# A 3x3 convolution in Winograd form: the first pair's store issued three PSUM copies later, and seven rows stored apart in another pair

## The chip, the cores and the metric

The kernel runs on one core of one Trainium2 chip. The time is the device time of one launch in microseconds (us), the median of several runs. A profile is one more execution, taken by the hardware profiler; its span runs from the core's first instruction to its last.

The names of the engines are those of the profile: PE (TensorE, matmuls), PEld (its weight loads), DVE (VectorE), ACT (ScalarE), POOL (GpSimd) and SP (SyncE). A "q" behind a name (SPq, ACTq) stands for that engine's sequencer, which waits and issues DMAs.

## What is computed

A convolution of 16 images with 64 input channels of 64 x 64 pixels, with a 3 x 3 kernel, a border of one zero pixel and 128 output channels, all in float32 in DRAM:

```python
batch, c_in, h, w, c_out = 16, 64, 64, 64, 128
x_pad = np.pad(x, ((0, 0), (0, 0), (1, 1), (1, 1)), mode='constant')
...
output[b, co] += weight[co, ci, kh, kw] * x_pad[b, ci, kh:kh+h, kw:kw+w]
```

The input is 16.8 MB, the output 33.6 MB, the weights 0.3 MB.

## The kernel before, in words

**Work and tiles.** Two images make a pair: 2 x 64 input channels fill the 128 partitions, and there are eight pairs. Each pair is computed in two halves (h = 0 and 1) of 32 output rows, so the main loop (L206) has 16 passes, n = 0 to 15. A half uses four PSUM tiles (pf1, pg1, pf2, pg2), which hold the vertical Winograd sums for 16 row pairs, in two blocks of eight. Three of them are copied to SBUF by ScalarE (`copied`, L180, recorded at L182: ux, ug, uy), ScalarE then casts the next half's rows to 16 bits (`cast`, L122, recorded at L124), VectorE makes three of the four output parts (L231 to L233), and ScalarE copies the fourth (L234). GpSimd makes the input sums and differences of the half after the next (`transforms`, L208; recorded at L106, L113 and L119).

**Homes.** One SBUF tile, `homes`, has nine slots of 16 KB per partition. An input pair takes one (X_HOME, L49), an output pair takes two that lie side by side, one for each of its images (O_HOME, L50). Pair 0's output lies in slots 5 and 6, which pair 3's output takes again, and later pair 6's. Pair 1's output lies in slots 3 and 4, which pair 4's takes again.

**DMAs.** SP issues the weights (L58), then the loads of pair 0 in two cuts, of pairs 1 and 2, and of pairs 3 and 4 in one DMA of 4096 KB (L68 to L72). The loads of pairs 5, 6 and 7 come later, behind the first halves of pairs 2, 3 and 4 (NEXT_LOADS, L53 and L237), because they need slots whose earlier inputs have been read. The output of a pair is stored by `store` (L187) once its second half is done. Pairs 0, 3 and 6 (BOTH, L51) are stored by one DMA of 4096 KB; the others by one DMA of 2048 KB for each image. ScalarE issues the store of pair 0 and SP all others. For one image, named by FEW (L52), the last seven rows are stored apart: one DMA for the first 57 rows of all 128 channels (1824 KB), one for the last seven rows of 124 channels (217 KB) and one for those of the last four channels (7 KB). In the kernel before this is pair 5, image 1 of the pair.

**What sets the order.** Every instruction is wrapped in `keep`, so each engine runs its instructions in the order of the program. An issue of a DMA stands in its engine's queue like any other instruction: it first waits for its data (for a store, the last of L231 to L234), and what stands behind it on that engine waits as well. In the kernel before ScalarE's queue reads, around the store of pair 0: the copy of L234 for n = 1, the issue at L192, then the three copies of L182 and the cast for n = 2. Within SP's queue the DMAs stand in this order: weights, five loads, the stores of pair 1, load 5, the stores of pair 2, load 6, the store of pair 3, load 7, the stores of pairs 4, 5, 6 and 7. The completion semaphores of all DMAs, ScalarE's among them, are eight, used in turn in program order: a DMA also waits until the one eight places before it has landed.

Of the kernel before, what the change touches and what calls it, by code (L numbers as in the profile page):

```python
# [15 lines left out]
def kernel(  # L16
# [32 lines left out]
    X_HOME = [0, 1, 2, 7, 8, 2, 7, 8]  # L49
    O_HOME = [5, 3, 0, 5, 3, 0, 5, 2]  # L50
    BOTH = (0, 3, 6)  # L51
    FEW = 5, 1, 7  # L52
    NEXT_LOADS = {(2, 0): 5, (3, 0): 6, (4, 0): 7}  # L53
    homes = slots.tile([128, 9, H, W], F32)
    xs = [homes[:, k, :, :] for k in X_HOME]
# [4 lines left out]
    def load(p, cuts=((0, H),)):  # L60
        for lo, hi in cuts:
            keep(
                nc.sync.dma_start(
                    xs[p][:, lo:hi, :], x_rows[128 * p : 128 * p + 128, lo:hi, :]
                )
            )
# [55 lines left out]
    def cast(p, h):  # L122
        t = cpool.tile([128, 17, W], F16, tag="xh", name="xh")
        keep(nc.scalar.copy(t, xs[p][:, C_ROW[h] : C_ROW[h] + 17, :]))  # L124
        return t

    def transforms(eng, p, h):
        return sums(eng, p, h), diffs(eng, p, h), outers(eng, p, h)
# [17 lines left out]
    def mms(tiles, terms, start, stop):  # L146
        n = 3 * len(terms)
        i = 0
        for wi, src, row in terms:
            for kw in (1, 0, 2):  # L150
                c_lo, c_hi = max(0, 1 - kw), min(W, W + 1 - kw)
                lo, hi = 0, RB
                at, step, rows = row
                while at + step * lo < 0:
                    lo += 1
                while at + step * (hi - 1) > rows - 1:
                    hi -= 1
                first, last = at + step * lo, at + step * (hi - 1)
                for b2 in range(2):
                    p0 = 64 * b2  # L160
                    keep(
                        nc.tensor.matmul(  # L162
                            tiles[:, b2, lo:hi, c_lo:c_hi],
                            Wt[p0 : p0 + 64, wi, kw, :],
                            src[
                                p0 : p0 + 64,
                                first : last + 1 : step,
                                c_lo + kw - 1 : c_hi + kw - 1,
                            ],
                            start=start and i == 0,  # L170
                            stop=stop and i == n - 1,
                            skip_group_check=not start,
                        )
                    )
                i += 1

    def acc():
        return psum.tile([128, 2, RB, W], F32, tag="acc", name="acc")

    def copied(tiles):  # L180
        ut = upool.tile([128, 2, RB, W], F32, tag="ut", name="ut")
        keep(nc.scalar.copy(ut, tiles))  # L182
        return ut
# [3 lines left out]
    def store(p, both):  # L187
        if p in BOTH:
            pair = out[2 * p : 2 * p + 2, :, :, :].rearrange("b c h w -> c b h w")

            eng = nc.scalar if p == 0 else nc.sync
            keep(eng.dma_start(pair, both))  # L192
            return
        for b2 in range(2):
            parts = [(0, CO, 0, H)]
            if (p, b2) == FEW[:2]:
                at = H - FEW[2]
                parts = [(0, CO, 0, at), (0, 124, at, H), (124, 4, at, H)]
            for c, n, lo, hi in parts:
                keep(  # L200
                    nc.sync.dma_start(
                        out[2 * p + b2, c : c + n, lo:hi, :], both[c : c + n, b2, lo:hi, :]
                    )
                )

    for n, (p, h) in enumerate(halves):  # L206
        if n + 2 < len(halves):
            tr[halves[n + 2]] = transforms(nc.gpsimd, *halves[n + 2])  # L208
        if h == 0:
            both = homes[:, O_HOME[p] : O_HOME[p] + 2, :, :]  # L210
            ov = both.rearrange("p b (j i) c -> p b j i c", i=2)
        ss, dd, ee = tr.pop((p, h))
        xc = xh.pop((p, h))
        jf, jg = RB * F_BLK[h], RB * G_BLK[h]
        sf, sg = jf - 16 * h, jg - 16 * h
        g_at = 2 * jg - C_ROW[h]

        pf1, pg1, pf2, pg2 = acc(), acc(), acc(), acc()
        mms(pf1, [(HP, ss, (sf, 1, 16))], True, True)
        ux = copied(pf1)  # L220
        mms(pg1, [(G1, ss, (sg, 1, 16))], True, True)
        ug = copied(pg1)
        mms(pf2, [(HM, dd, (0, 1, RB))], True, True)
        uy = copied(pf2)
        if n + 1 < len(halves):
            xh[halves[n + 1]] = cast(*halves[n + 1])
        mms(pg2, [(G01, xc, (g_at, 2, 17)), (G2, xc, (g_at + 2, 2, 17))], True, True)
        mms(pf1, [(G0, ee, (0, 2, 16))], False, True)
        mms(pg1, [(G21, xc, (g_at + 1, 2, 17)), (G0, xc, (g_at - 1, 2, 17))], False, True)
        mms(pf2, [(G2, ee, (1, 2, 16))], False, True)  # L230
        keep(nc.vector.tensor_add(ov[:, :, jg : jg + RB, 1, :], pg2, ug))  # L231
        keep(nc.vector.tensor_add(ov[:, :, jf : jf + RB, 0, :], pf1, uy))  # L232
        keep(nc.vector.tensor_sub(ov[:, :, jf : jf + RB, 1, :], ux, pf2))  # L233
        keep(nc.scalar.copy(ov[:, :, jg : jg + RB, 0, :], pg1))  # L234
        if h == 1:
            store(p, both)
        if (p, h) in NEXT_LOADS:  # L237
            load(NEXT_LOADS[p, h])

# [29 lines left out]
```

## Time and profile before

| what | value |
|---|---|
| time, median of 3 runs | 126.86 us (126.43 to 127.62) |
| the profiled execution's own time | 126.95 us |
| its span | 125.2 us |
| PE busy | 95.7 us (76%) |
| POOL busy | 90.5 us (72%) |
| ACT busy | 81.4 us (65%) |
| DVE busy | 63.9 us (51%) |
| moved by DMA | 50.77 MB, mean 406 GB/s |
| last instruction of the computing engines | DVE L233, 102.66 to 103.88 us |

Times inside the profile are counted from the start of the span. The profile's page cuts the span into 40 equal slices of 3.13 us; a table by stretches gives for each stretch the busy time of every engine, the granted TensorE clock (PEclk), the DMA share (the time of all DMA packets that start in the stretch, over 16 engines) and the GB/s that these packets moved. Packets are counted where they start, so that neighbouring stretches of one microsecond trade some per cent, and a share can stand a little over 1. A row of the DMA queues gives packets, megabytes and share: q1 holds what SP issued, q10 what ScalarE issued, q8 and q14 fetch instructions. Besides these views the trace has a record of each DMA packet (start, duration, size, queue), without the number of the DMA engine; where the text uses it, it says so.

### The profile page before, as it was taken

To read this page: it belongs to the slowest core of one execution; us is meant where nothing else is said; L and a number is where in the kernel's file an instruction comes from. 1 tells how busy PE (TensorE), PEld (TensorE's weight loads), DVE (VectorE), ACT (ScalarE), POOL (GpSimd) and SP (SyncE) were. 2 spreads that over 40 slices of the span, in tenths; PEclk is the share of its full clock that TensorE was granted. 3 is DMA by queue.
4 is the path that set the end of the run, shared out by engine and by line. 5 is a ranking of instruction groups with operands and counts; after the bars stand their busy time and mean duration, and the time that the engine had idled before them with its cause. 6 is when DMAs were issued, how large, how long until landed. Compare 5 with 4: busy or idle time off the path is not lost.

```text
span 125.2 us, 2157 instructions
## 1 busy us (share of the span) xinstructions
PE 95.7 (76%) x873; PEld 50.5 (40%) x873; DVE 63.9 (51%) x56; ACT 81.4 (65%) x86; POOL 90.5 (72%) x52
## 2 busy tenths in 40 slices
PE   0349999999999999999999999999999980000000
PEld 0224455455555555555555555555555530000000
DVE  0199657374939375674839393746647392000000
ACT  4457598599797978889897979788897940000000
POOL 2209999999999999999999999999999400000000
PEclk9999999999999999999999999999999997555555
DMA  4999999999999999999999999999999999999981
GB/s 125 375 454 424 429 429 429 435 335 419 424 429 435 435 419 429 403 437 440 437 411 382 440 424 419 429 440 424 435 419 431 426 414 436 429 440 435 419 372 58
DMA packets 3826, 50.77 MB, mean 406 GB/s; under 512 B 360, under 2 KB 488, under 8 KB 744
## 3 DMA queue, kind: packets, MB, share of 16 engines
q1 hardware_dynamic: 3544, 46.43, 88.6%
q10 hardware_dynamic: 272, 4.19, 7.9%
q8 instruction: 7, 0.11, 0.3%
q14 instruction: 3, 0.02, 0.0%
HBM read 17.07 MB, written 33.55 MB: 405 GB/s over the span
## 4 chain that ended last, share of the span: by engine, by line
PE 76%; DVE 3%; DMA 2%; POOL 1%; ACT 0%; issue 0%; DVEq 0%
PE acc L162 76%; DMA w_raw<-in_weight_dram 2%; DVE homes L233 1%; DVE ss L106 1%; POOL w L78 1%; DVE th L133 0%; DVE Wt L134 0%; PE wp L95 0%; ACT g0h L131 0%; DVEq L134 0%
## 5 line engine op out<-in xcount | busy, mean ns | idle before, releaser
L162 PEld LDWEIGHTS <-Wt 64*128 64x128 f16 x864 | 49.6, 96 | 47.0 <-issue 3.7
L182 ACT COPY ut<-acc 128x1024 f32<-128x1024 f32 x48 | 45.7, 1020 | 6.3 <-PE acc L162 6.3
L162 PE MATMUL acc<-xh,Wt 64*128 64x504 f16 (+3 forms) x384 | 46.3, 372 | 0.0
L106 POOL TENSOR_TENSOR ss<-homes 128x1024 f16<-128x1024 f32 x15 | 35.5, 2369 | 4.7 <-DMA homes<-in_x_dram 4.7
L231 DVE TENSOR_TENSOR homes<-acc,ut 128x1024 f32<-128x1024 f32 x16 | 19.6, 1225 | 32.2 <-PE acc L162 29.7
L119 POOL TENSOR_TENSOR ee<-homes 128x1024 f16<-128x1024 f32 x15 | 35.6, 2375 | 0.0
L162 PE MATMUL acc<-ss,Wt 64*128 64x504 f16 (+1 forms) x192 | 24.9, 392 | 2.3 <-DVE ss L106 2.3
L162 PE MATMUL acc<-ee,Wt 64*128 64x504 f16 (+1 forms) x192 | 26.5, 377 | 0.0
L234 ACT COPY homes<-acc 128x1024 f32<-128x1024 f32 x16 | 16.2, 1015 | 11.3 <-PE acc L162 10.7
L233 DVE TENSOR_TENSOR homes<-ut,acc 128x1024 f32<-128x1024 f32 x16 | 19.5, 1220 | 2.0 <-PE acc L162 1.4
L113 POOL TENSOR_TENSOR dd<-homes 128x512 f16<-128x512 f32 x15 | 20.2, 1347 | 0.0
L232 DVE TENSOR_TENSOR homes<-acc,ut 128x1024 f32<-128x1024 f32 x16 | 19.4, 1215 | 0.0
L124 ACT CAST xh<-homes 128x1088 f16<-128x1088 f32 x16 | 17.9, 1120 | 0.0
L162 PE MATMUL acc<-dd,Wt 64*128 64x504 f16 (+1 forms) x96 | 13.9, 392 | 0.0
L95 PE MATMUL wp<-ident,w 128*128 128x128 f16 x9 | 1.1, 309 | 4.6 <-POOL w L78 4.6
L133 DVE SCALAR_TENSOR_TENSOR th<-wp,g0h 128x384 f32<-128x384 f32 x1 | 0.6, 557 | 5.7 <-ACT g0h L131 5.7
L95 PEld LDWEIGHTS <-w 128*128 128x128 f16 x9 | 0.9, 158 | 4.6 <-POOL w L78 4.6
L119 DVE TENSOR_TENSOR ee<-homes 128x1024 f16<-128x1024 f32 x1 | 2.6, 2622 | 0.0
L78 POOL CAST w<-w_raw 128x576 f16<-128x576 f32 x1 | 0.7, 662 | 2.5 <-DMA w_raw<-in_weight_dram 2.5
L79 ACT CAST w<-w_raw 128x576 f16<-128x576 f32 x1 | 0.7, 672 | 1.8 <-DMA w_raw<-in_weight_dram 1.8
L79 ACT ACT_TABLE_LOAD x1 | 1.3, 1283 | 0.7 <-PEq L253 0.7
L106 DVE TENSOR_TENSOR ss<-homes 128x1024 f16<-128x1024 f32 x1 | 1.2, 1216 | 0.0
(15 smaller groups left out, 5.7 us busy)
## 6 DMA issues: line engine op xcount, KB each, us to landing
out_dram<-homes SPq DMA_DIRECT2D x9, 2048.0 KB, 17.5
homes<-in_x_dram SPq DMA_DIRECT2D x5, 2048.0 KB, 18.8
out_dram<-homes SPq DMA_DIRECT2D x2, 4096.0 KB, 22.2
homes<-in_x_dram SPq DMA_DIRECT2D x1, 4096.0 KB, 30.4
out_dram<-homes ACTq DMA_DIRECT2D x1, 4096.0 KB, 18.6
out_dram<-homes SPq DMA_DIRECT2D x1, 1824.0 KB, 23.6
homes<-in_x_dram SPq DMA_DIRECT2D x1, 1088.0 KB, 5.5
homes<-in_x_dram SPq DMA_DIRECT2D x1, 960.0 KB, 7.4
```

The lines of the kernel that those rows point to most:

```text
L79: keep(nc.scalar.copy(w16[:, 1, :], w_raw))
L95: keep(nc.tensor.matmul(wps[kh][:, k * CO : k * CO + CO], w16[:, :, 3 * kh + k :: 9], ident))
L106: keep(eng.tensor_add(t, v[:, j : j + 16, 0, :], v[:, j : j + 16, 1, :]))
L113: keep(eng.tensor_sub(t, v[:, j : j + RB, 1, :], v[:, j : j + RB, 0, :]))
L119: keep(eng.tensor_sub(t, xs[p][:, r - 1 : r + 15, :], xs[p][:, r + 1 : r + 17, :]))
L124: keep(nc.scalar.copy(t, xs[p][:, C_ROW[h] : C_ROW[h] + 17, :]))
L162: nc.tensor.matmul(tiles[:, b2, lo:hi, c_lo:c_hi], Wt[p0 : p0 + 64, wi, kw, :], src[p0 : p0 + 64, first : last + 1 : step, c_lo + kw - 1 : ...
L182: keep(nc.scalar.copy(ut, tiles))
L231: keep(nc.vector.tensor_add(ov[:, :, jg : jg + RB, 1, :], pg2, ug))
L232: keep(nc.vector.tensor_add(ov[:, :, jf : jf + RB, 0, :], pf1, uy))
L233: keep(nc.vector.tensor_sub(ov[:, :, jf : jf + RB, 1, :], ux, pf2))
L234: keep(nc.scalar.copy(ov[:, :, jg : jg + RB, 0, :], pg1))
```

## The change

ScalarE issues the store of pair 0 in pass n = 2, behind the copies ux, ug and uy of that pass and ahead of the cast for the next one, instead of at the end of pass n = 1. And the image whose last seven rows are stored apart is pair 1, image 0, instead of pair 5, image 1. The number of DMAs, their sizes and everything else stay the same.

```diff
-    FEW = 5, 1, 7
+    FEW = 1, 0, 7
...
         mms(pf2, [(HM, dd, (0, 1, RB))], True, True)
         uy = copied(pf2)
+        if n == 2:
+
+            store(0, first)
         if n + 1 < len(halves):
             xh[halves[n + 1]] = cast(*halves[n + 1])
...
         keep(nc.scalar.copy(ov[:, :, jg : jg + RB, 0, :], pg1))
-        if h == 1:
+        if h == 1 and p > 0:
             store(p, both)
+        if p == 0:
+            first = both
```

## The prediction, made before the changed kernel ran

> **What bounds the kernel now.** I read the engines' busy times and the 40 slices first, then the end of the chain of waits, then the table by stretches, then the queues, and last the timelines of ScalarE and SP around the two edits.
>
> The page, engines, slices and queues:
>
> ```profile
> PE 95.7 (76%) x873; PEld 50.5 (40%) x873; DVE 63.9 (51%) x56; ACT 81.4 (65%) x86; POOL 90.5 (72%) x52
> DMA  4999999999999999999999999999999999999981
> GB/s 125 375 454 424 429 429 429 435 335 419 424 429 435 435 419 429 403 437 440 437 411 382 440 424 419 429 440 424 435 419 431 426 414 436 429 440 435 419 372 58
> DMA packets 3826, 50.77 MB, mean 406 GB/s; under 512 B 360, under 2 KB 488, under 8 KB 744
> q1 hardware_dynamic: 3544, 46.43, 88.6%
> q10 hardware_dynamic: 272, 4.19, 7.9%
> ```
>
> No computing engine is full, while the DMA engines are full in every slice but the first and the last two. The chain of waits ends with the compute:
>
> ```profile
> 8.09 94.56 PE acc L162 x864
> ...
> 102.66 1.22 DVE homes L233
> ```
>
> At 103.88 us everything is computed, and the span still has 21.3 us of stores: at 430 GB/s that is pair 7's 4.19 MB, issued at 103.95, and about as much again that was already queued. So SP's stores are some 10 us ahead of the DMA engines at the end, and compute may slip by that much for nothing. What bounds is how much the 16 DMA engines carry and how long they run below their rate. The table by stretches says where that is:
>
> ```profile
> 0.00:6.00 6.00, 1.15 (x9) 0.92 (x9) 0.32 (x1) 2.80 (x4) 1.36 (x7) 1.00 0.71 244
> 6.00:24.00 18.00, 15.91 (x130) 7.70 (x132) 13.62 (x14) 11.98 (x15) 14.86 (x7) 1.00 1.02 432
> 24.00:30.00 6.00, 6.00 (x58) 3.16 (x56) 3.48 (x3) 6.00 (x7) 6.00 (x4) 1.00 1.00 380
> 30.00:66.00 36.00, 36.00 (x342) 19.35 (x340) 21.85 (x19) 30.58 (x33) 36.00 (x20) 1.00 1.01 426
> 66.00:69.00 3.00, 3.00 (x31) 1.57 (x29) 2.83 (x3) 2.10 (x3) 3.00 (x3) 1.00 1.01 399
> 69.00:120.00 51.00, 33.63 (x316) 17.84 (x312) 21.82 (x19) 27.91 (x29) 29.25 (x15) 0.85 1.01 430
> 120.00:122.00 2.00, 0.00 (x0) 0.00 (x0) 0.00 (x0) 0.00 (x0) 0.00 (x0) 0.50 0.73 311
> 122.00:123.00 1.00, 0.00 (x0) 0.00 (x0) 0.00 (x0) 0.00 (x0) 0.00 (x0) 0.50 0.42 180
> 123.00:124.00 1.00, 0.00 (x0) 0.00 (x0) 0.00 (x0) 0.00 (x0) 0.00 (x0) 0.50 0.04 16
> ```
>
> The last number of a row is GB/s. Against 432, the undisturbed rate: 50.77 MB take 117.5 us. The start loses 6 x (432 - 244)/432 = 2.61, the stretch 24 to 30 loses 6 x 52/432 = 0.72, 30 to 66 loses 0.50, 66 to 69 loses 0.23, 69 to 120 loses 0.24; from 120 to 124 the engines finish one after the other, which loses (242 + 252 + 416)/432 = 2.11; and 1.2 us follow the last packet. Sum 125.1 of the span's 125.2. Every edit is now asked which of these terms it moves. The profiled execution took 126.95 us, 1.75 more than its span and 0.09 above the median of the three runs.
>
> **Edit 1, the store of pair 0 later.**
>
> ```profile
> 16.91 2.85 ACT L182 COPY ut<-acc 128x1024 f32<-128x1024 f32 x3 [0.28 <-PE acc L162]
> ...
> 21.37 1.01 ACT L234 COPY homes<-acc 128x1024 f32<-128x1024 f32 x1 [0.62 <-PE acc L162]
> 23.33 0.42 ACTq L192 DMA_DIRECT2D out_dram<-homes  x1
> 23.79 2.84 ACT L182 COPY ut<-acc 128x1024 f32<-128x1024 f32 x3 [1.41 <-PE acc L162]
> 26.51 1.12 ACT L124 CAST xh<-homes 128x1088 f16<-128x1088 f32 x1
> ```
>
> *ScalarE.* The issue waits for DVE L233 (22.02 + 1.22 = 23.24), and the copies of n = 2 stand behind it. Passes come every 5.75 us, so without it these copies start at 16.91 + 5.75 = 22.66 and end at 25.5; the store then issues at 25.5 instead of 23.33 (2.2 later; its data are long ready), and the cast starts at 25.9 instead of 26.51. DVE L231, which waited 2.51 us for ACT at 25.75, gets its input about 0.5 earlier. All of it lies beside a PE that never pauses, and compute ends 10 us before it matters: cost and gain 0. Were that cover gone, 0.42 us of issue ahead of the cast would be the price.
>
> *DMA.* The same 4096 KB queue 2.2 us later. Three things can follow. (a) A gap: if the loads ran out first, all 16 engines would idle. The loads issued at the start are 10.78 MB; at 432 GB/s with the start's 2.61 us they end at 27.6. The only issue into idle engines is that of the weights: issued at 0.73, landed 3.04 later, 0.7 of it the 0.295 MB itself, so at most 2.3 us pass from issue to data; the packet records put the first weight packet at 1.75, 1.0 after its issue. The store's first packet could then come between 26.5 and 27.8. Gap between 0 and 0.2; I take 0, since the record is the direct one. The Trainium skill, "DMA: Bandwidth & Descriptors", section "Latency and other measured facts", gives about 600 ns to the first byte for this path; behind the issue's 0.42 that makes an estimate of 26.5 and no gap, as the packet record has it. (b) The loss of 0.72 in 24 to 30. It falls where the loads hand over to this store: the packet records show the first store packet at 27.1, each engine carrying four more load packets after the store could have come (24.3), and those last load packets taking up to 1.4 us where 0.61 is usual. With the issue 2.2 us later, 2.2/0.61 = 3.6 fewer load packets are left, about 2 of 5.5. The nearest other hand-overs are load 6 to pair 3's store, 0.23 in 66 to 69, and load 7 to pair 4's, near 0 (428 GB/s in 82 to 90). So the loss afterwards lies between 0 and 0.72; I take 0.72 x 2/5.5 = 0.26, by the nearest row 0.23. (c) Who ends last. The time is that of the last engine, not of their mean. By following the packets I find that the engines lost between 0.1 and 1.2 each in that stretch, and the one that ended last (its last packet at 123.85) lost 0.49. So the gain of (b) at the end is 0.49 x 3.5/5.5 = 0.31, with ends 0 and 1.2.
>
> *What waits for this store.* Pair 3 writes into slots 5 and 6, first at 48.41 (DVE L231); the store landed at 23.33 + 18.6 = 41.9, so 2.2 later still clears it by 4. Load 6, eight places behind it in the turn of the semaphores, issues at 51.3. Nothing.
>
> **Edit 2, the seven rows.** Of q1's 3544 packets 3200 are data; the other 344 are 16 for each of 21 DMAs and 4 for each of the two small ones, so those run on four engines each. 128 packets lie between 512 B and 2 KB: the 128 rows of 1792 B, 32 on each of four engines. By the packet records one takes 74 ns, a 57-row packet 545 and a 64-row one 611. So four engines get 32 x 0.074 = 2.4 us more, and all 16 give back 8 x 0.066 = 0.5, before and after alike: over the whole run each engine carries the same. What moves is when: four engines run 2.4 us later from about 43 us on, not from about 101. That would cost if something waited for a landing. Following the packets, these four were among the first to land load 7 (82.0 to 82.9; the last engine 84.6; POOL needs it at 86.46) and pair 3's store (77.1 to 78.0; last 79.7; pair 6 writes over it at 82.94): 1.9 later they are level with the last, and no wait appears. On SP the two small issues now stand between pair 1's two images:
>
> ```profile
> 34.92 1.17 SPq L201 DMA_DIRECT2D out_dram<-homes  x2
> 39.56 0.34 SPq L63 DMA_DIRECT2D homes<-in_x_dram  x1
> ```
>
> In pair 5 four such issues took 2.88 us, so these end by 37.8, before load 5 can issue at 39.56, and pair 1's second image, 1.7 later, still queues behind a store that lands at 41.9. The semaphores' turn shifts by two for what lies between; the DMA eight places back has landed by then for each (the tightest is load 6 on pair 0's store, above). Cost 0, ends -0.2 and +0.2: the four engines meet the hand-over at 66 to 69 at another moment, and that term is 0.23.
>
> **Sum.** 126.95 - 0.31 + 0 = 126.64 for the profiled execution, 126.55 on the scale of the median: 126.5.
>
> **Rivals.** *Order only.* The loss in 24 to 30 belongs to any hand-over and moves along with the store: 126.9. For it: the same bytes, and the table shows a dip at 66 to 69 too, where nothing is issued. Against it: at 82 to 90 a hand-over shows none. This is also what follows from the Trainium skill's "DMA: Bandwidth & Descriptors", "Issuing engines are not separate DMA queues": the same 16 engines, whoever issues, so only order can change; the trace agrees that q10's packets only take their place among q1's.
>
> *Slower: the store comes too late.* In the kernel before 3.75 us passed from its issue (23.33) to its first packet (27.1). If that is the delay of a 4096 KB store and not the four load packets ahead of it, its first packet comes at 25.5 + 3.75 = 29.25, the loads end at 27.6, and 1.65 us of all engines are lost; less the 0.72 that goes, +0.9, 127.8, and 128.5 if the 0.72 stays. It decides from a delay of 2.1 us on. Against it: the weights' 1.0.
>
> *More than computed.* The whole 0.72 goes and the engine that ends last is one that lost 1.2, and the hand-over at 66 to 69 loses nothing since four engines are out of step: 126.95 - 1.2 - 0.2 = 125.5. For it: the spread from 0.1 to 1.2. Against it: the engine that ended last lost 0.49.
>
> **How the numbers follow.** Forecast 0.42 (its own range 125.9 to 127.1), order only 0.24, too late 0.20, more than computed 0.14. A measurement of this kernel can tell about 1%, 1.27 us, from no change: faster is below 125.6, slower above 128.1. Faster takes the last case's 0.14 and 0.04 of the forecast's lower edge, 0.18; slower takes the part of the late store in which the dip stays too, 0.14; the rest is 0.68. The range 125.5 to 128.1 leaves out the dearer half of the late store and the edge beyond 125.5.
>
> **What would show it.** Right: ScalarE's issue at about 25.5 behind three copies that start at 22.66; the table at 24 to 30 above 400 GB/s; 120 to 124 as before; the 1792-B packets near 43 us. Wrong: a DMA share well under 1 near 28 (a gap), the dip moved whole to 27 to 30, a POOL or DVE wait on a DMA, or a longer tail from 120 on, which would say that moving the rows did change who ends last.

## The result, and the profile after

The changed kernel takes 127.43 us (median of 22 runs, 127.03 to 129.22) against 126.82 of the kernel before on the same chips; the ratio is 1.005, 95% interval 1.0033 to 1.0066. That is 0.6 us slower: the forecast, 0.3 us faster, had the wrong sign, though the time lies within its range. (Ratios leave disturbed executions out; medians include them.) The profiled execution took 127.35 us, its span is 125.6.

Three rows of the page after, in the order of the ones shown before: the GB/s of the 40 slices, the DMA packets and ScalarE's queue. Bytes, packets and small packets are the same to the last digit:

```profile
GB/s 133 368 455 433 418 423 433 438 324 428 438 418 426 412 451 423 342 423 423 425 425 423 428 428 433 423 428 428 433 428 438 423 428 423 433 428 438 433 360 57
DMA packets 3826, 50.77 MB, mean 404 GB/s; under 512 B 360, under 2 KB 488, under 8 KB 744
...
q10 hardware_dynamic: 272, 4.19, 7.8%
```

Slice 9 still has its dip (324, before 335), slice 17 has a new one (342 at 50 to 53 us, before 403), and slice 22 (66 to 69) has lost its own (423, before 382). The table by stretches of the changed kernel, columns as before:

```profile
0.00:6.00 6.00, 1.15 (x9) 0.92 (x9) 0.52 (x1) 2.81 (x4) 1.37 (x7) 1.00 0.72 247
6.00:24.00 18.00, 15.95 (x132) 7.90 (x134) 13.66 (x14) 13.35 (x15) 14.75 (x7) 1.00 1.01 432
24.00:30.00 6.00, 5.98 (x58) 2.83 (x56) 3.58 (x3) 5.10 (x7) 6.00 (x4) 1.00 1.01 377
30.00:66.00 36.00, 36.00 (x342) 16.49 (x338) 22.00 (x19) 30.39 (x33) 36.00 (x20) 1.00 1.00 418
66.00:69.00 3.00, 3.00 (x32) 1.37 (x28) 2.82 (x3) 2.10 (x3) 3.00 (x3) 1.00 1.01 426
69.00:120.00 51.00, 33.49 (x316) 15.13 (x310) 21.68 (x19) 27.77 (x29) 29.39 (x16) 0.88 1.01 430
120.00:122.00 2.00, 0.00 (x0) 0.00 (x0) 0.00 (x0) 0.00 (x0) 0.00 (x0) 0.50 0.84 360
122.00:123.00 1.00, 0.00 (x0) 0.00 (x0) 0.00 (x0) 0.00 (x0) 0.00 (x0) 0.50 0.42 180
123.00:124.00 1.00, 0.00 (x0) 0.00 (x0) 0.00 (x0) 0.00 (x0) 0.00 (x0) 0.50 0.23 98
```

The same sum against 432 GB/s, in us: 117.5 for the bytes, 2.57 at the start, 0.76 in 24 to 30 (before 0.72), 1.17 in 30 to 66 (before 0.50), 0.04 in 66 to 69 (0.23), 0.24 to 120, 1.69 from 120 to 124, and 1.6 behind 124 (1.2 before; the last packet now ends at 124.41, before at 123.85): 125.6, the span. The new time is in 30 to 66, and within it in one place. Before, then after:

```profile
30.00:50.00 20.00, 20.00 (x190) 10.75 (x188) 12.32 (x11) 16.89 (x18) 20.00 (x12) 1.00 1.01 428
50.00:56.00 6.00, 6.00 (x60) 3.23 (x58) 3.89 (x4) 4.88 (x6) 6.00 (x4) 1.00 1.02 427
56.00:66.00 10.00, 10.00 (x98) 5.38 (x96) 5.64 (x6) 8.81 (x10) 10.00 (x6) 1.00 1.00 421
```

```profile
30.00:50.00 20.00, 20.00 (x192) 9.17 (x188) 12.45 (x11) 16.56 (x18) 20.00 (x12) 1.00 1.00 425
50.00:56.00 6.00, 6.00 (x60) 2.73 (x56) 3.89 (x4) 5.01 (x6) 6.00 (x4) 1.00 1.00 384
56.00:66.00 10.00, 10.00 (x98) 4.59 (x94) 5.66 (x6) 8.81 (x10) 10.00 (x6) 1.00 1.00 424
```

From 50 to 56 us the rate fell from 427 to 384 GB/s: 6 x 43/432 = 0.60 us. There load 5 hands over to pair 2's stores. Its DMA share stays at 1.00, so no engine idled: packets took longer. The packet records say so too: of the 16 KB packets of loads and stores that start between 46 and 58 us, 8 took over 0.68 us before and 35 take so long now, and 22 of these start between 51.0 and 52.6. Nor does a computing engine wait for a DMA after the start; these are all such waits of the changed kernel:

```profile
POOL ss L106 <- DMA homes<-in_x_dram: 5.0, 1, 5.0
...
POOL w L78 <- DMA w_raw<-in_weight_dram: 2.3, 1, 2.3
...
ACT w L79 <- DMA w_raw<-in_weight_dram: 1.6, 1, 1.6
```

Following the packets from one to the next on each engine gives the same picture by engine (an inference, since the records carry no engine number). The four engines with the 1792-B packets finish pair 1's second image at 49.3 to 49.7 instead of 47.8 to 48.0, so they begin load 5 about 1.7 us late. Their load packets in 50 to 56 then take up to 1.45 us in place of 0.61, and most of the other twelve have slow ones at the same moment. In the kernel before these four lost about 0.1 us each between 30 and 62, now 0.9 to 1.6; the other twelve lost 0.4 on average before, 0.7 now. And the four, which ended at 122.6 to 123.5 before, now end last, at 123.6 to 124.4.

ScalarE around the store of pair 0, after:

```profile
16.66 2.84 ACT L182 COPY ut<-acc 128x1024 f32<-128x1024 f32 x3 [0.28 <-PE acc L162]
...
21.11 1.01 ACT L236 COPY homes<-acc 128x1024 f32<-128x1024 f32 x1 [0.62 <-PE acc L162]
22.41 1.93 ACT L182 COPY ut<-acc 128x1024 f32<-128x1024 f32 x2 [0.28 <-PE acc L162]
23.77 0.42 ACTq L191 DMA_DIRECT2D out_dram<-homes  x1
24.23 1.03 ACT L182 COPY ut<-acc 128x1024 f32<-128x1024 f32 x1
```

The reader is to see that the issue stands ahead of the start of the third copy, at 23.77: 0.44 us later than before, not 2.2. The sequencer had handed the third copy to the engine, which was still busy with the second (22.41 to 24.34 for the first two), and issued the DMA without waiting for either. The pass itself came 0.26 us earlier in this execution. Counted from the start of the copy ahead of it (L234 before, L236 after), the issue comes 2.66 us behind instead of 1.96, so the edit's own delay is 0.70 us. That is less than what separates one execution from the next: in the ten kernels that keep the early store, it is issued between 22.68 and 23.90.

### The profile page after: what moved, and what is told of

Read it like the earlier page. It is cut to its first block, busy times and chain, and to the rows that moved or that the text cites. A ratio compares the mean times of both kernels' runs of the same rounds, so it can differ in the third digit from the quotient of the medians.

```text
span 125.6 us, 2162 instructions
## 1 busy us (share of the span) xinstructions
PE 95.6 (76%) x873; PEld 44.6 (36%) x873; DVE 64.3 (51%) x56; ACT 81.5 (65%) x86; POOL 90.5 (72%) x52
## 4 chain that ended last, share of the span: by engine, by line
PE 75%; DMA 4%; DVE 2%; SPq 0%; issue 0%
PE acc L162 75%; DMA homes<-in_x_dram 4%; DVE ss L106 1%; DVE homes L235 1%; SPq L58 0%
## 5 line engine op out<-in xcount | busy, mean ns | idle before, releaser
L162 PEld LDWEIGHTS <-Wt 64*128 64x128 f16 x864 | 43.7, 95 | 53.0 <-issue 3.4
L162 PE MATMUL acc<-xh,Wt 64*128 64x504 f16 (+3 forms) x384 | 45.7, 371 | 0.0
L236 ACT COPY homes<-acc 128x1024 f32<-128x1024 f32 x16 | 16.2, 1013 | 11.9 <-PE acc L162 11.3
L234 DVE TENSOR_TENSOR homes<-acc,ut 128x1024 f32<-128x1024 f32 x16 | 19.4, 1214 | 0.0
```

The source lines that it names most:

```text
L162: nc.tensor.matmul(tiles[:, b2, lo:hi, c_lo:c_hi], Wt[p0 : p0 + 64, wi, kw, :], src[p0 : p0 + 64, first : last + 1 : step, c_lo + kw - 1 : ...
```

## The experiments

The theory after the result (R): the rows cost. Four engines that carry them in pair 1 are behind when load 5 hands over to pair 2's stores, and lose there. The main rival (S): the later store costs. Each kernel is told by its difference from the kernel before, and each ratio is against the kernel before, timed beside it. Of each kernel one execution was profiled.

### Edit 1 alone (late_only, late_again)

```diff
+        if n == 2:
+            store(0, first)
...
-        if h == 1:
+        if h == 1 and p > 0:
             store(p, both)
+        if p == 0:
+            first = both
```

> Edit 1 alone: the store of pair 0 in pass n = 2, the seven rows still in pair 5. Theory R (the rows cost: four engines that carry them early lag when load 5 hands over to pair 2's store, lose time there and end last): ScalarE's issue comes at 23.8, only 0.4 later than before, so the time is that of before, ratio 0.998 to 1.002, 126.6 to 127.1 us. Rival S (the later store costs, by moving the dip of 24 to 30): ratio 1.004 to 1.006, 127.3 to 127.6 us.

Measured: 126.79 us, ratio 1.0013 (0.9986 to 1.004). That speaks against rival S, whose range begins where this interval ends. But the profile also showed a smaller dip at the first hand-over and a larger loss at load 5's, so that a gain given back was possible (theory G); these are its rows for 24 to 30 and 50 to 56:

```profile
24.00:30.00 6.00, 5.98 (x58) 2.90 (x56) 3.58 (x3) 5.10 (x7) 6.00 (x4) 1.00 1.01 410
50.00:56.00 6.00, 6.00 (x60) 2.83 (x58) 3.89 (x5) 5.00 (x6) 6.00 (x4) 1.00 1.02 411
```

The same kernel was therefore run once more.

> Edit 1 alone, once more. Theory G: 24 to 30 near 410 GB/s and 50 to 56 near 411, ratio 0.998 to 1.002. Rival O: 24 to 30 at 371 to 393 and 50 to 56 at 420 or more, the same ratio.

Measured: 126.70 us, ratio 0.999 (0.9966 to 1.0014), and

```profile
24.00:30.00 6.00, 5.97 (x60) 2.58 (x56) 3.58 (x3) 5.09 (x6) 6.00 (x4) 1.00 1.02 385
50.00:56.00 6.00, 6.00 (x60) 2.74 (x58) 3.72 (x5) 5.09 (x6) 6.00 (x4) 1.00 1.00 426
```

The time excludes rival S. 385 lies among the kernels with the early store (371 to 393), so theory G is no rule; 410 was one execution. What the two profiles do not share is when the store was issued: at 24.45 in the first and at 23.26 in the second, since the pass came 1.2 us earlier there. By the packet records 18 packets of 16 KB took over 0.68 us around this hand-over in the first, 34 in the second, and 28 in the kernel before. So a store issued 1.1 us later than before may shrink the dip; one execution does not show it, and 24.09 in a kernel further below gave 374. In time edit 1 is order only.

### Edit 2 alone (rows_only)

```diff
-    FEW = 5, 1, 7
+    FEW = 1, 0, 7
```

> Edit 2 alone: the rows in pair 1, image 0, the store of pair 0 as before. Theory R: all of the 0.5%, ratio 1.004 to 1.006, 127.3 to 127.6 us; the four engines with the rows have their last packets later than the other twelve, and the stretch 50 to 55 loses as in the changed kernel. Rival S: as before, ratio 0.998 to 1.002.

Measured: 127.36 us, ratio 1.0053 (1.0031 to 1.0076): the whole of the change. The stretch of load 5's hand-over loses exactly as in the changed kernel:

```profile
50.00:56.00 6.00, 6.00 (x60) 3.20 (x56) 3.76 (x4) 5.10 (x6) 6.00 (x4) 1.00 1.01 384
```

By the packets the four engines end at 123.8 to 124.2. One of the twelve, the slow engine of the next section, ends at 124.1 too (123.9 before), so the four alone do not set this time.

### The rows in pair 4, and nowhere (rows_p4, rows_none)

```diff
-    FEW = 5, 1, 7
+    FEW = 4, 0, 7
```

> The kernel before with the rows in pair 4, image 0: behind load 7, the last load, but earlier than pair 5. Theory R: no load follows the rows, so the four engines lose nothing by lagging: as before, ratio 0.998 to 1.002. Rival B (rows stored earlier cost in themselves, the earlier the more): between before and changed, ratio 1.001 to 1.004.

Measured: 126.95 us, ratio 1.0024 (1.0001 to 1.0046), 422 GB/s in 50 to 56. That lies in rival B's range and just above theory R's: less than half of the cost, with an interval that reaches down to almost none. Its profiled execution is the fastest of all profiled ones (126.62 us), so no trace shows where the 0.24% comes from. Position alone is not excluded by this kernel; the packets of the kernels without hand-overs, below, speak against it.

```diff
-    FEW = 5, 1, 7
+    FEW = 9, 0, 7
```

> The kernel before with no rows stored apart: every store runs on all 16 engines. By the packet records of before the four engines would end 2.4 us earlier and the other twelve 0.5 later, so the last packet comes 0.5 later: ratio 1.003 to 1.005, 127.2 to 127.5 us, under each theory. Should it be as before, the last engine is not what sets the time, and theory R falls.

Measured: 127.32 us, ratio 1.0049 (1.0034 to 1.0065), a time as computed, and without any dip at load 5:

```profile
50.00:56.00 6.00, 6.00 (x60) 3.21 (x58) 3.89 (x4) 5.10 (x6) 6.00 (x4) 1.00 1.01 430
```

That fits a time set by the engine that ends last: with the work spread evenly half of the engines end before 122 by the packets, and the slowest at 123.9. It does not show it in full: the last packet of the kernel before ended at 123.85, so the 0.5 us are in the medians and not between these two profiled executions (127.19 and 126.95 us). In each of the two the last is one slow engine: its stores take 634 to 672 ns a packet instead of 611 while the computing engines run, and the usual 611 afterwards and for loads.

### Three rows instead of seven (rows3_p1)

```diff
-    FEW = 5, 1, 7
+    FEW = 1, 0, 3
```

> The kernel before with three rows instead of seven stored apart, in pair 1, image 0: the four engines lag by about 1.1 us less, and the other twelve carry four rows more, 0.3 us by the packet records. Theory R (the cost is that the four end last): they end about 1 us before the slowest of the twelve, which ends 0.3 later than before: ratio 1.001 to 1.003. Rival B (rows this early cost in themselves): 1.004 or more.

Measured: 127.16 us, ratio 1.003 (1.0007 to 1.0053), 427 GB/s in 50 to 56. As theory R computed it, and with a point it had not: with a lag of about half the hand-over of load 5 loses no more than in the kernel before. What is left fits the slowest engine's four rows more (0.3 us), but its profiled execution (126.75 us) does not show them: its last packet ends at 123.67, before 123.85.

### The rows behind load 5 (rows_p2)

```diff
-    FEW = 5, 1, 7
+    FEW = 2, 0, 7
```

> The kernel before with the rows in pair 2, image 0: behind load 5, ahead of load 6. Theory L (whichever load comes next, engines that lag lose at its hand-over to a store): the stretch 50 to 56 is back at about 427 GB/s, 66 to 69 loses more than before (below 399 GB/s), the four engines end last: ratio 1.003 to 1.006, 127.1 to 127.5 us. Rival H (only the hand-over of load 5 is touchy): 50 to 56 and 66 to 69 as before, ratio 0.998 to 1.002.

Measured: 127.64 us, ratio 1.0057 (1.0036 to 1.0078). The loss has moved to the next hand-over, from load 6 to pair 3's store; rows for 50 to 56 and 66 to 69:

```profile
50.00:56.00 6.00, 6.00 (x60) 3.23 (x58) 3.72 (x5) 5.09 (x6) 6.00 (x4) 1.00 0.99 419
66.00:69.00 3.00, 3.00 (x31) 1.57 (x29) 2.54 (x3) 2.10 (x3) 3.00 (x3) 1.00 1.01 322
```

322 where the kernel before has 399, and 419 where the kernel with the rows ahead of load 5 has 384. Theory L holds: it is the hand-over that comes next behind the rows, not load 5 as such. By the packets the four engines end at 123.6 to 124.3, last again.

### No hand-over left (nohand_p5, nohand_p1, nohand_p5_again, nohand_late)

```diff
+    spare = nc.dram_tensor("spare", [3, 128, H, W], F32, kind="Internal").ap()
+
+    def again(q):
+        keep(nc.sync.dma_start(spare[q - 5, :, :, :], xs[q]))
...
-            load(NEXT_LOADS[p, h])
+            again(NEXT_LOADS[p, h])
```

> The kernel before (rows in pair 5), with loads 5, 6 and 7 replaced by stores of the same slots and sizes to a spare tensor in DRAM; pairs 5 to 7 so compute on the inputs of pairs 2 to 4, and those outputs are not the reference's. Same bytes on the same queue, but after the first loads only stores, so no hand-over is left behind the first. By the hand-over theory the stretches 50 to 56 and 66 to 69 run at about 428 GB/s; slots wait less, so the time is 0.1 to 0.5 us below before: 126.4 to 126.9 us.

> The same with the rows in pair 1, image 0; its outputs of pairs 5 to 7 are not the reference's either. Hand-over theory: the four engines still run 2 us behind, but no load loses by it, so the time is that of the kernel with the rows in pair 5 within 0.25% (0.3 us). Rival B (rows stored this early cost in themselves): 0.4 to 0.6% more than that kernel, 0.5 to 0.8 us.

Measured: 127.31 us with the rows in pair 5 and 127.33 with the rows in pair 1; against the kernel before 1.0043 (1.0028 to 1.0059) and 1.0032 (1.0018 to 1.0047). The two agree. Alone this does not refute rival B, since one slow engine ends both kernels at 124.2 and would hide 0.6 us on the others; the packets do. Only 3 packets of 16 KB that start between 46 and 58 us take over 0.68 us in either kernel, against 35 in the changed kernel. The row for 50 to 56 of the kernel with the rows in pair 1:

```profile
50.00:56.00 6.00, 6.00 (x60) 3.18 (x56) 3.88 (x4) 4.85 (x5) 6.00 (x4) 1.00 1.01 430
```

By the packets its four engines run about 2 us behind most of the others from 49 us on, as in the changed kernel, and yet lose no more than in the other (at most 0.12 us each in 30 to 62 for the three that can be told from the slow engine); these three end at 123.1 to 123.3, where the four of nohand_p5 end at 122.5 to 123.2. So rows stored early cost these engines next to nothing in themselves, and rival B falls. That both kernels are slower than the kernel before, not faster as expected, fits the one slow engine: it now stores where it loaded, 24 packets more at the slower rate, and ends last at 124.2.

> The kernel with stores in place of loads 5, 6 and 7, the rows in pair 5 and the early store, once more, as the yardstick on the same chip (outputs of pairs 5 to 7 are not the reference's): ratio 1.003 to 1.006, 24 to 30 at 371 to 393 GB/s.

> Stores in place of loads 5, 6 and 7 (outputs of pairs 5 to 7 are not the reference's), rows in pair 5, and the store of pair 0 issued as in the changed kernel. Theory G (the gain of the later store is real, and is given back at load 5 where there is one): 24 to 30 near 410 GB/s, and 0.2 to 0.3% below the same kernel with the early store. Rival O (order only): 371 to 393 GB/s as in all looks with the early store, and the same time within 0.15%.

Measured: 127.38 us, ratio 1.0031 (1.0007 to 1.0056), 380 GB/s in 24 to 30, with the early store, and 127.26 us, 1.0023 (0.9997 to 1.0049), 374 GB/s, with the late one. The intervals are too wide to exclude theory G's 0.2% by the time; the dip speaks against it, since 374 is not near 410, with an issue at 24.09. Rival O, order only, once more.

### The store truly later (store_end2, store_n3)

Because the sequencer runs ahead of the copies, the change's delay was small. Two kernels delay the store in earnest.

```diff
         keep(nc.scalar.copy(ov[:, :, jg : jg + RB, 0, :], pg1))
-        if h == 1:
+        if n == 2:
+            store(0, first)
+        if h == 1 and p > 0:
             store(p, both)
+        if p == 0:
+            first = both
```

> Rows as before; ScalarE issues the store of pair 0 behind the last copy of pass n = 2, at about 26.5 by the trace of the changed kernel, some 3 us later than before. The prediction's reason (a later issue leaves fewer load packets ahead of it, and the dip of 24 to 30 goes): above 415 GB/s in 24 to 30 if the store's first packet comes in time; ratio 0.995 to 0.999. Rival G (what is saved there is lost at the next hand-over, load 5's): 24 to 30 above 400 GB/s but 50 to 56 below 415, ratio 0.999 to 1.003. Rival T (too late): a gap at 27.5 to 28.5 with a DMA share below 0.8 and a ratio above 1.004.

Measured: 128.40 us, ratio 1.0123 (1.0097 to 1.0149). ScalarE issued at 27.64, the first packet came at 28.57 by the packet records, and all but one of the engines had run out of loads at 27.5 to 28.1. Rows of 24 to 30 and 50 to 56:

```profile
24.00:30.00 6.00, 6.00 (x60) 3.09 (x58) 3.58 (x3) 5.10 (x7) 6.00 (x4) 1.00 0.91 388
50.00:56.00 6.00, 6.00 (x60) 3.13 (x58) 3.89 (x5) 4.85 (x5) 6.00 (x4) 1.00 0.97 348
```

In 24 to 30 the share of 0.91 says that engines idled (0.51 in 27 to 28, 0.65 in 28 to 29), by the packets 0.5 to 1.2 us on nearly every engine. No packet of loads or stores was slow there: with no load left beside the store the dip is gone. But the engines, which had all started anew at 28.6, now came to load 5 in step and lost there some 2 us each, on the last packets of pair 1's stores (1.2 us instead of 0.61) and on the last ones of the load. Rival T is right, and so is the mechanism of rival G, at a higher price.

```diff
-        if n == 2:
+        if n == 3:
             store(0, first)
```

(against late_only)

> Rows as before; the store of pair 0 goes out among the copies of pass n = 3, at about 29.5. All the first loads have then ended (27.6), so the DMA engines idle until the first packet, about 1 us behind the issue: 30.5 less 27.6, near 3 us, less the dip of 0.7 which has no load left to fall on: plus 2.2, 129.0 us, ratio 1.015 to 1.02. If the delay from issue to first packet is nearer the 3.75 us of the kernel before, plus 5, ratio 1.035 to 1.045.

Measured: 130.44 us, ratio 1.0264 (1.0236 to 1.0292), between the two expectations. The issue came at 30.33, the first packet 0.94 behind it:

```profile
28.00:31.00 3.00, 3.00 (x32) 1.52 (x30) 1.52 (x2) 2.72 (x4) 3.00 (x2) 1.00 0.01 5
49.00:52.00 3.00, 3.00 (x32) 1.37 (x28) 2.75 (x3) 2.34 (x3) 3.00 (x3) 1.00 1.03 333
...
54.00:58.00 4.00, 4.00 (x40) 1.85 (x38) 3.00 (x3) 3.10 (x4) 4.00 (x3) 1.00 0.98 299
```

The gap is 3.5 us by the packets, the dip of 0.7 is gone, and the two turns around load 5 lose 3 x 99/432 + 4 x 133/432 = 1.9 us. 3.5 - 0.7 + 1.9 = 4.7 against a span that is 4.0 longer; where the other 0.7 is won was not followed. One landing so late also makes DVE wait 3.0 us (pair 6's output over pair 3's), but computing is done at 105.4 of 129.2.

### One hand-over fewer (joined)

```diff
-        if h == 1:
+        if h == 1 and p != 2:
             store(p, both)
+        if p == 2:
+            held = both
         if (p, h) in NEXT_LOADS:
             load(NEXT_LOADS[p, h])
+        if (p, h) == (3, 0):
+            store(2, held)
```

> The kernel before with pair 2's stores issued behind load 6 instead of ahead of it, so that loads 5 and 6 run one after the other and one hand-over from loads to stores falls away (52 us). If each hand-over costs by itself, the loss of 66 to 69 (0.23 us) and that near 52 become one: ratio 0.995 to 1.000. If the cost lies with how many loads are still in flight on engines that lag, one hand-over with a wider spread costs as much: ratio 0.999 to 1.004. The stores of pair 2 come 4.9 us later, landing near 68, and pair 5 writes over their slots at 71: no wait.

Measured: 128.77 us, ratio 1.0143 (1.0104 to 1.0182), slower than either expectation. Load 6 waits for its slot until about 51.4, and with pair 2's stores behind it the DMA engines had nothing else: the row 52 to 54 shows a share of 0.86. Rows of 52 to 60:

```profile
52.00:54.00 2.00, 2.00 (x22) 1.03 (x18) 0.66 (x1) 1.91 (x3) 2.00 (x2) 1.00 0.86 340
54.00:56.00 2.00, 2.00 (x22) 1.13 (x20) 1.33 (x2) 1.93 (x3) 2.00 (x2) 1.00 1.05 369
56.00:58.00 2.00, 2.00 (x22) 1.04 (x19) 1.83 (x2) 1.17 (x2) 2.00 (x2) 1.00 1.01 254
58.00:60.00 2.00, 2.00 (x22) 1.03 (x18) 0.41 (x1) 2.00 (x3) 2.00 (x2) 1.00 0.85 295
```

And the one hand-over left, in 56 to 60, reached behind a gap, loses 2 x 178/432 + 2 x 137/432 = 1.5 us where the two of the kernel before lost 0.3 together.

No version was found that beats the kernel before beyond its interval.

## Why the prediction was wrong, point by point

**What bounds.** Right. The sum by stretches closes on both kernels (125.1 of 125.2, 125.6 of 125.6), the DMA share stays at 1.00 or more from 6 to 120, and compute's end does not matter.

**Edit 1, when the store is issued.** Wrong. The step took "behind three copies" for the end of the third copy, 25.5; the trace has 23.77. Here the DMA issue needed no result of the copies ahead of it, and it waited only until the sequencer had handed those to the engine: it stands 0.46 us ahead of the start of the third.

**Edit 1, its worth.** Wrong by its whole size: -0.31 was forecast, and the two runs alone give ratios of 1.0013 and 0.999. With 0.70 us of delay about one load packet less stands ahead of the store, so by the prediction's own scale only 0.72 x (0.70/0.61)/5.5 = 0.15 us was to be had; these runs could not tell that from nothing. The idea behind it is shown right only at its extreme: in store_end2 and store_n3 the store comes when the loads are all but over, and no load packet is slow in 24 to 30. It is useless there: a gap and larger losses at the next turns replace the dip. That the delay from issue to first packet is about 1 us and not 3.75 was right (0.93 and 0.94 us). The Trainium skill's page "DMA: Bandwidth & Descriptors", section "Latency and other measured facts", with its 600 ns to the first byte behind 0.41 of issue, gives an estimate of 1.0; the trace agrees.

**Edit 2.** This is the step that failed: "Cost 0, ends -0.2 and +0.2". It was true that the two places cost each engine the same bytes, that SP loses nothing (its four issues end at 38.71, not by 37.8, still ahead of load 5 at 39.66), and that no instruction waits for a late landing. What it left out is that a lag of four engines changes how long load packets take at the next hand-over from loads to stores. The prediction saw that these engines "meet the hand-over at 66 to 69 at another moment", and bounded it by what that hand-over cost before (0.23), and never asked about the hand-over between, load 5's, which cost next to nothing before. The runs: 0.60 us in 50 to 56, of which edit 2 alone has all; 0.2 came back at 66 to 69. One of the prediction's own signs of being wrong appeared as well, the longer tail: 98 GB/s in 123 to 124 where there were 16. Of the 0.71 us between the 126.64 forecast for the profiled execution and its 127.35, 0.31 are edit 1's missing gain and 0.40 edit 2's cost, as far as single executions show it. A dip that a trace does not show is no bound on what a changed order makes there.

**The rivals.** Order only fits edit 1. Too late was wrong in both its premises, an issue at 25.5 and 3.75 us from there to the first packet: the change issues at 23.77, and into idle engines 0.94 us pass. A gap would open from an issue at about 26.7 on (27.6 less 0.94); store_end2, issued at 27.64, has it and costs 1.2%, part of it at load 5. That the change as a whole would be slower by 0.5% stood in no rival.

**What stays open.** Why packets slow down at a turn from loads to stores, and why a lag of 1.7 us on four engines costs there while one of about half of that does not. The runs show that the cost of the rows needs both the lag and the hand-over. They also show that a lag is not the only way to lose there: the first hand-over loses 0.7 us with no rows ahead of it, load 5's lost 0.3 in the first execution of edit 1 alone (411 GB/s), and engines in step behind an idle gap lose most. A cause in the memory or in the DMA engines was not tried.

## What to carry to other kernels

When the DMA engines are the bound, ask two things of an edit that moves a transfer: which of the 16 engines then ends last, and what the engines that fall behind meet next. In this kernel work that only some engines carry belongs behind the last turn from loads to stores (1.005 and 1.006 ahead of a turn, 1.002 behind the last). And a DMA issued behind other instructions on ScalarE did not wait here for them to finish (issued at 27.64 in store_end2, 0.06 behind the start of a copy of 1.02); if a delay is the point, read in the trace when the issue really stands, and by how much that moves from one execution to the next.

## What the runs showed of the hardware that was not expected

- Packets of 16 KB take 0.61 us throughout, but the last one to four ahead of a turn between loads and stores often take 0.8 to 1.5, in the changed kernel on nearly all 16 engines within 2 us; with the engines in step it hits both directions of the turn, about 2 us an engine around load 5 in store_end2.
- In the kernel before, the store on ScalarE's queue got its first packet on an engine only after four or five more load packets, and from then on the two queues took turns packet by packet. That is why 3.75 us passed there and 0.94 with idle engines.
- One of the 16 engines stores 4 to 10% slower (634 to 672 ns a packet) as long as compute runs, in every kernel that was followed; in the kernel before it ended last, at 123.85. Storing seven rows apart takes 14 KB off each of twelve engines, this one among them, and gives 43 KB to each of four others; without that the kernel is 0.49% slower.
